# Top-2 gate scaling: groups of 66 and 62 rows per partition in place of 65 and 63

## The chip, the cores and the metric

The kernel runs on one core of one Trainium2 chip. The time is the device time in microseconds (us) of one launch; the figure compared is the median of several runs. Sizes written KB are kibibytes here: a row of `x` is 512 float32 values, or 2 KB, and a row pair of the output is 4 KB.

## The reference

For each of 16 x 1024 tokens there is a row of 512 float32 values and 8 router logits. The two largest softmax probabilities of a token, normalised to sum to one, scale two copies of its row:

```python
probs = np.exp(router_logits - logits_max)
probs = probs / np.sum(probs, axis=-1, keepdims=True)
topk_indices = np.argsort(probs, axis=-1)[..., -k:]
topk_probs = np.take_along_axis(probs, topk_indices, axis=-1)
topk_probs = topk_probs / np.sum(topk_probs, axis=-1, keepdims=True)
x_expanded = x[:, :, np.newaxis, :].repeat(k, axis=2)
return (x_expanded * topk_probs[..., np.newaxis]).astype(np.float32)
```

The smaller of the two weights comes first. With `k = 2` the two weights are the sigmoid of minus and of plus the difference of the two largest logits. 32 MiB of rows come in and 64 MiB go out, so that nearly all of the work is moving data.

## The kernel before

There are 16384 rows, 128 per partition. They are cut into two groups of consecutive rows, `GROUPS = [65, 63]`: in a group of G rows, partition p holds the G consecutive rows from p x G on. A load or store of some rows of a group therefore moves one contiguous run for each of the 128 partitions, and the runs of neighbouring partitions lie G rows apart in memory: 130 KB (G = 65) or 126 KB (G = 63) for loads, twice that, 260 or 252 KB, for stores.

Three buffers lie in the on-chip memory. `xs` has one slot of 2 KB per partition for each row of the larger group. `osp` has `L = 18` slots of 4 KB for row pairs of the output. `WA` holds the weights. A load puts row r of group g into `xs` slot `BASE[g] + r`. A store takes its row pairs either from `osp` or from `xs`: `place` lays the pairs over `xs` slots whose rows have been used, two slots for each pair, so that the multiplication writes partly over its own input.

The list `LOADS` gives the rows of each load, and `STORES` gives for each store its first row, its number of rows, the buffer and the first slot. For each store the main loop issues one VectorE multiplication (line 133), which spreads a row over both weights, and then one store (line 145). Where a store from `osp` slot 0 comes again, its multiplication is cut in two after `FREE[g]` rows: the first part needs only slots that are free early, the second part waits until an earlier store has left the slots behind them.

All loads and all stores but the first go through SyncE's DMA queue (SP), in the order of the program; the first store, of 3 rows, goes through ScalarE's (ACT). SP waits for the multiplication before it issues a store, and for a store to have landed before it issues a load into the same slots. The order on SP is: loads of 2 and 4 rows of group 0, the two loads of logits (lines 125 and 126), the loads of 28 and 31 rows, four stores, the three loads of group 1, four stores. In this document these transfers have names, in the order in which they are issued:

- L1 to L4: the loads of group 0; S0 is the 3-row store on the ACT queue.
- S1 to S4: the stores of group 0 on the SP queue, from rows 3, 18, 34 and 49.
- L5 to L7: the loads of group 1, of 16, 16 and 31 rows. L5 and L6 wait for S2 to have left its `xs` slots, L7 for S4.
- S5 to S8: the stores of group 1, from rows 0, 16, 32 and 47.

The weights come from twelve small VectorE operations on the logits and two ScalarE sigmoids, all in `top2_weights`, which use `osp` as their workspace and are over before the first store.

Of the kernel before, what the change touches and what calls it, by code (L numbers as in the profile page):

```python
# [1 line left out]

# [4 lines left out]

F32 = mybir.dt.float32
ALU = mybir.AluOpType
ACTF = mybir.ActivationFunctionType  # L10
P = 128


def top2_weights(nc, WA, dlt, room, logits, E):

    tt = nc.vector.tensor_tensor
    hi, lo, n = None, None, E  # L20
    while n > 1:
        n //= 2
        if hi is None:
            a, b = logits[:, :, 0:n], logits[:, :, n : 2 * n]
            nhi, nlo = room(n), b
            tt(nhi, a, b, op=ALU.max)  # L26
            tt(nlo, a, b, op=ALU.min)  # L27
        else:
            a, b = hi[:, :, 0:n], hi[:, :, n : 2 * n]
            nhi, nlo, tmp = room(n), room(n), room(n)  # L30
            tt(tmp, lo[:, :, 0:n], lo[:, :, n : 2 * n], op=ALU.max)  # L31
            tt(nlo, a, b, op=ALU.min)  # L32
            tt(nlo, nlo, tmp, op=ALU.max)  # L33
            tt(nhi, a, b, op=ALU.max)  # L34
        hi, lo = nhi, nlo
    tt(dlt, hi[:, :, 0], lo[:, :, 0], op=ALU.subtract)  # L36
    nc.scalar.activation(WA[:, :, 0], dlt, ACTF.Sigmoid, scale=-1.0)  # L37
    nc.scalar.activation(WA[:, :, 1], dlt, ACTF.Sigmoid, scale=1.0)  # L38

GROUPS = [65, 63]

LOADS = [[2, 4, 28, 31], [16, 16, 31]]
BASE = [0, 1]

STORES = [
    [(0, 3, "osp", 0), (3, 15, "osp", 3), (18, 16, "xs", 0), (34, 15, "osp", 0), (49, 16, "xs", 33)],
    [(0, 16, "osp", 2), (16, 16, "xs", 0), (32, 15, "osp", 0), (47, 16, "xs", 32)],
]  # L50

L = 18

FREE = [3, 2]


@with_exitstack
def kernel(
    ctx: ExitStack,
    tc: tile.TileContext,  # L60
    x: bass.AP,
    router_logits: bass.AP,
    k: bass.AP,
    out: bass.AP,
):
    nc = tc.nc
    B, S, D = x.shape
    E = router_logits.shape[-1]
    N = B * S
    assert int(k) == 2 and E == 8 and N == P * sum(GROUPS)  # L70
    M = N // P

    x_v, o_v, rl_v = [], [], []
    t0 = 0
    for n in GROUPS:
        t1 = t0 + P * n
        x_v.append(
            x.rearrange("b s d -> (b s) d")[t0:t1].rearrange("(p m) d -> p m d", p=P)
        )
        o_v.append(  # L80
            out.rearrange("b s k d -> (b s) k d")[t0:t1].rearrange(
                "(p m) k d -> p m k d", p=P
            )
        )
        rl_v.append(
            router_logits.rearrange("b s e -> (b s) e")[t0:t1].rearrange(
                "(p m) e -> p m e", p=P
            )
        )
        t0 = t1  # L90

    wpool = ctx.enter_context(tc.tile_pool(name="wpool", bufs=1))
    xs = wpool.tile([P, max(GROUPS), D], F32)
    osp = wpool.tile([P, L, 2, D], F32)
    WA = wpool.tile([P, M, 2], F32)
    dlt = wpool.tile([P, M], F32)


    flat = osp.rearrange("p l k d -> p (l k d)")
    taken = [0]  # L100

    def room(n):
        o = taken[0]
        taken[0] += M * n
        return flat[:, o : o + M * n].rearrange("p (m n) -> p m n", n=n)

    logits = room(E)

    def place(where, at, n):

        if where == "osp":
            return osp[:, at : at + n]
        return xs[:, at : at + 2 * n, :].rearrange("p (r k) d -> p r k d", k=2)

    m0 = 0
    for g, G in enumerate(GROUPS):
        x0, r = BASE[g], 0
        for n in LOADS[g]:
            tc.keep_in_program_order(
                nc.sync.dma_start(xs[:, x0 + r : x0 + r + n, :], x_v[g][:, r : r + n, :])  # L120
            )
            r += n
            if g == 0 and r == 6:
                n0 = GROUPS[0]
                tc.keep_in_program_order(nc.sync.dma_start(logits[:, :n0], rl_v[0]))  # L125
                tc.keep_in_program_order(nc.sync.dma_start(logits[:, n0:], rl_v[1]))  # L126
                top2_weights(nc, WA, dlt, room, logits, E)
        assert r == G
        for r, n, where, at in STORES[g]:
            og = place(where, at, n)  # L130
            again = where == "osp" and at == 0 and r > 0
            for a, b in [(0, FREE[g]), (FREE[g], n)] if again else [(0, n)]:
                nc.vector.tensor_tensor(  # L133
                    og[:, a:b],
                    xs[:, x0 + r + a : x0 + r + b, :]
                    .unsqueeze(2)
                    .to_broadcast([P, b - a, 2, D]),
                    WA[:, m0 + r + a : m0 + r + b, :]
                    .unsqueeze(3)
                    .to_broadcast([P, b - a, 2, D]),  # L140
                    op=ALU.mult,
                )

            queue = nc.scalar if g == r == 0 else nc.sync
            tc.keep_in_program_order(queue.dma_start(o_v[g][:, r : r + n], og))  # L145
        m0 += G


# [1 line left out]
_INS = ['x', 'router_logits', 'k']  # L150
_OUTS = [((16, 1024, 2, 512), 'float32')]

_NUMBERS = {'k': 2}


# [26 lines left out]
```

## Time and profile before

| what | value |
|---|---|
| median of 3 runs | 240.08 us (239.9 to 240.19) |
| span of the profiled execution, first to last instruction | 238.1 us |
| median less that span | 1.98 us |
| VectorE busy | 141.9 us, 60% of the span |
| bytes read and written | 34.08 MB and 67.11 MB |
| mean over the span | 425 GB/s |

The profile is of one execution, of which it records the span alone; what lies around it is taken as the difference between the median and the span. A line of the profile that names `out_dram<-osp` is a store from `osp`, one that names `xs<-in_x_dram` is a load. "SPq" is the sequencer that issues transfers, and its rows last only as long as the issue. The time from issue to landing holds the time that the transfer stands in the queue behind earlier ones. "DMA share" is the mean busy share of the core's 16 DMA engines; in a short stretch it can go over 1.00, since a packet is counted as a whole.

### The profile page before, as it was taken

The numbers are of one execution on the slowest core, as the hardware profiler recorded it, in microseconds if no ns is written. First come the engines' busy times: TensorE is split into PE (matmuls) and PEld (weight loads), VectorE is DVE, ScalarE is ACT, GpSimd is POOL, SyncE is SP. The second block draws the span as 40 slices with busy tenths as digits, with TensorE's granted clock in tenths as the row PEclk, the third lists the DMA queues.
The fourth block names the chain that finished last, engine by engine and source line by source line (L and its number), as shares of the span: only waits on it lengthen the run. The fifth ranks groups of instructions, "written<-read, shape, count | busy, mean of one in ns | idle before, by whom it ended". The sixth has DMA issues, their size and how long they took to land.

```text
span 238.1 us, 105 instructions
## 1 busy us (share of the span) xinstructions
DVE 141.9 (60%) x22; ACT 1.8 (1%) x3; POOL 0.2 (0%) x4
## 2 busy tenths in 40 slices
DVE  0560499999689999100000799999406999950000
ACT  2000000000000000000000000000000000000000
POOL 0000000000000000000000000000000000000000
DMA  7979998979998999989899999898999989989894
GB/s 249 537 337 526 419 429 376 506 330 495 407 451 363 517 392 434 495 352 528 352 440 440 429 446 491 363 495 374 484 396 418 462 352 506 475 351 517 352 528 176
DMA packets 2593, 101.19 MB, mean 425 GB/s; under 512 B 289, under 2 KB 417, under 8 KB 673
## 3 DMA queue, kind: packets, MB, share of 16 engines
q1 hardware_dynamic: 2448, 99.62, 97.2%
q10 hardware_dynamic: 144, 1.57, 1.5%
q14 instruction: 1, 0.00, 0.0%
HBM read 34.08 MB, written 67.11 MB: 425 GB/s over the span
## 4 chain that ended last, share of the span: by engine, by line
DMA 48%; DVE 40%; SPq 1%; issue 0%; DVEq 0%
DVE osp L133 25%; DMA xs<-in_x_dram 25%; DMA out_dram<-osp 22%; DVE xs L133 14%; SPq L120 0%; SPq L126 0%; SPq L125 0%; SPq L145 0%; DVEq L133 0%
## 5 line engine op out<-in xcount | busy, mean ns | idle before, releaser
L133 DVE TENSOR_TENSOR osp<-xs,WA 128x3072 f32<-128x3072 f32 (+5 forms) x7 | 69.4, 9909 | 61.2 <-DMA xs<-in_x_dram 47.2
L133 DVE TENSOR_TENSOR xs<-xs,WA 128x16384 f32<-128x16384 f32 x4 | 68.9, 17224 | 0.1
L26 DVE TENSOR_TENSOR osp<-osp 128x512 f32<-128x512 f32 x1 | 0.7, 691 | 8.4 <-DMA osp<-in_router_logits_dram 8.4
L37 ACT ACT_TABLE_LOAD x1 | 1.3, 1283 | 0.7 <-PEq L163 0.7
L27 DVE TENSOR_TENSOR osp<-osp 128x512 f32<-128x512 f32 x1 | 0.7, 691 | 0.0
L31 DVE TENSOR_TENSOR osp<-osp 128x256 f32<-128x256 f32 (+1 forms) x2 | 0.7, 350 | 0.0
L32 DVE TENSOR_TENSOR osp<-osp 128x256 f32<-128x256 f32 (+1 forms) x2 | 0.7, 350 | 0.0
L34 DVE TENSOR_TENSOR osp<-osp 128x256 f32<-128x256 f32 (+1 forms) x2 | 0.7, 349 | 0.0
L33 DVE TENSOR_TENSOR osp<-osp 128x256 f32<-128x256 f32 (+1 forms) x2 | 0.7, 348 | 0.0
L37 ACT ACTIVATE WA<-dlt 128x128 f32<-128x128 f32 x1 | 0.3, 314 | 10.3 <-DVE dlt L36 10.3
L36 DVE TENSOR_TENSOR dlt<-osp 128x128 f32<-128x128 f32 x1 | 0.3, 293 | 0.0
L38 ACT ACTIVATE WA<-dlt 128x128 f32<-128x128 f32 x1 | 0.3, 298 | 0.0
L163 POOL MEMSET const-bfloat16-1.0<- 128x1 bf16 x1 | 0.1, 102 | 0.0
L163 POOL MEMSET const-uint8-127<- 128x1 uint8 x1 | 0.1, 101 | 0.0
L163 POOL MEMSET const-float32-0.0<- 128x1 f32 x1 | 0.1, 99 | 0.2 <-issue 0.2
L163 POOL MEMSET const-float32-1.0<- 128x1 f32 x1 | 0.1, 98 | 0.0
## 6 DMA issues: line engine op xcount, KB each, us to landing
out_dram<-osp SPq DMA_DIRECT2D x3, 7680.0 KB, 23.3
xs<-in_x_dram SPq DMA_DIRECT2D x2, 7936.0 KB, 41.3
xs<-in_x_dram SPq DMA_DIRECT2D x2, 4096.0 KB, 40.3
xs<-in_x_dram SPq DMA_DIRECT2D x1, 7168.0 KB, 24.4
out_dram<-osp ACTq DMA_DIRECT2D x1, 1536.0 KB, 26.9
xs<-in_x_dram SPq DMA_DIRECT2D x1, 1024.0 KB, 5.8
xs<-in_x_dram SPq DMA_DIRECT2D x1, 512.0 KB, 3.8
osp<-in_router_logits_dram SPq DMA_DIRECT2D x1, 260.0 KB, 6.0
```

Of the source, the lines that this page charges most:

```text
L26: tt(nhi, a, b, op=ALU.max)
L27: tt(nlo, a, b, op=ALU.min)
L31: tt(tmp, lo[:, :, 0:n], lo[:, :, n : 2 * n], op=ALU.max)
L32: tt(nlo, a, b, op=ALU.min)
L33: tt(nlo, nlo, tmp, op=ALU.max)
L34: tt(nhi, a, b, op=ALU.max)
L36: tt(dlt, hi[:, :, 0], lo[:, :, 0], op=ALU.subtract)
L37: nc.scalar.activation(WA[:, :, 0], dlt, ACTF.Sigmoid, scale=-1.0)
L38: nc.scalar.activation(WA[:, :, 1], dlt, ACTF.Sigmoid, scale=1.0)
L133: nc.vector.tensor_tensor(og[:, a:b], xs[:, x0 + r + a : x0 + r + b, :] .unsqueeze(2) .to_broadcast([P, b - a, 2, D]), WA[:, m0 + r + a : ...
L163: nc = _bacc.Bacc("TRN2", target_bir_lowering=False, num_devices=1)
```

## The change

Only constants at the head of the file change. Group 0 gets 66 rows per partition and group 1 gets 62. L4 loads 32 rows in place of 31 and L7 loads 30 in place of 31. S3 stores 16 rows in place of 15 and S8 stores 15 in place of 16. S4 starts one row later, and lies in `xs` slots 34 to 65 in place of 33 to 64. Group 1 is loaded from `xs` slot 0 on, where it was slot 1. `xs` grows by one slot, 2 KB per partition. The runs of neighbouring partitions now lie 132 and 124 KB apart for loads, 264 and 248 KB for stores. The two loads of logits split at 66 in place of 65. The number and order of instructions and transfers on each engine, and what each waits for, stay as they were; of the multiplications the second part of S3's is one row longer and S8's one row shorter.

```diff
-GROUPS = [65, 63]
+GROUPS = [66, 62]
 
-LOADS = [[2, 4, 28, 31], [16, 16, 31]]
-BASE = [0, 1]
+LOADS = [[2, 4, 28, 32], [16, 16, 30]]
+BASE = [0, 0]
 
 STORES = [
-    [(0, 3, "osp", 0), (3, 15, "osp", 3), (18, 16, "xs", 0), (34, 15, "osp", 0), (49, 16, "xs", 33)],
-    [(0, 16, "osp", 2), (16, 16, "xs", 0), (32, 15, "osp", 0), (47, 16, "xs", 32)],
+    [(0, 3, "osp", 0), (3, 15, "osp", 3), (18, 16, "xs", 0), (34, 16, "osp", 0), (50, 16, "xs", 34)],
+    [(0, 16, "osp", 2), (16, 16, "xs", 0), (32, 15, "osp", 0), (47, 15, "xs", 32)],
 ]
```

## The prediction

> **What bounds the kernel now.** I first read the page's head, then the strip of the DMA engines in 40 slices, the share of each queue, and one long stretch of the table of windows (its last two columns are the DMA share and GB/s).
>
> ```profile
> span 238.1 us, 105 instructions
> DVE 141.9 (60%) x22; ACT 1.8 (1%) x3; POOL 0.2 (0%) x4
> ...
> DMA  7979998979998999989899999898999989989894
> ...
> q1 hardware_dynamic: 2448, 99.62, 97.2%
> q10 hardware_dynamic: 144, 1.57, 1.5%
> ...
> 8.00:232.00 224.00, 141.91 (x22) 0.51 (x2) 0.00 (x0) 1.00 1.00 433
> ```
>
> The reader is to see that the two data queues keep the 16 DMA engines busy for 97.2 + 1.5 = 98.7% of 238.1 us, which is 235.0 us, and that from 8 to 232 us the share is 1.00 at 433 GB/s. VectorE works in 60% of the span. The chain that ended last seems to say something else:
>
> ```profile
> DMA 48%; DVE 40%; SPq 1%; issue 0%; DVEq 0%
> ...
> 194.54 17.22 DVE xs L133
> ```
>
> It gives 40% to VectorE, because it follows one instruction back at a time. Whether those multiplications bind is decided by whether the queue still holds work when each store is issued. For that I put beside the issue times on SP (first column)...
>
> ```profile
> 43.17 0.35 SPq L145 DMA_DIRECT2D out_dram<-osp  x1
> 60.43 0.34 SPq L145 DMA_DIRECT2D out_dram<-xs  x1
> 79.09 0.33 SPq L145 DMA_DIRECT2D out_dram<-osp  x1
> 96.35 0.33 SPq L145 DMA_DIRECT2D out_dram<-xs  x1
> 96.73 26.77 SPq L120 DMA_DIRECT2D xs<-in_x_dram  x3
> 149.96 0.34 SPq L145 DMA_DIRECT2D out_dram<-osp  x1
> 167.22 0.34 SPq L145 DMA_DIRECT2D out_dram<-xs  x1
> 194.53 0.33 SPq L145 DMA_DIRECT2D out_dram<-osp  x1
> 211.79 0.33 SPq L145 DMA_DIRECT2D out_dram<-xs  x1
> ```
>
> ...the time from issue to landing (last column), asked of the view of DMA issues for a short stretch around each issue: S1, S2, S3, S4, L5, L7, S5, S6, S7, S8 from top to bottom.
>
> ```profile
> out_dram<-osp SPq DMA_DIRECT2D x1, 7680.0 KB, 22.9
> out_dram<-xs SPq DMA_DIRECT2D x1, 25.0
> out_dram<-osp SPq DMA_DIRECT2D x1, 7680.0 KB, 24.4
> out_dram<-xs SPq DMA_DIRECT2D x1, 26.8
> xs<-in_x_dram SPq DMA_DIRECT2D x1, 4096.0 KB, 35.9
> xs<-in_x_dram SPq DMA_DIRECT2D x1, 7936.0 KB, 37.9
> out_dram<-osp SPq DMA_DIRECT2D x1, 30.5
> out_dram<-xs SPq DMA_DIRECT2D x1, 32.5
> out_dram<-osp SPq DMA_DIRECT2D x1, 7680.0 KB, 23.3
> out_dram<-xs SPq DMA_DIRECT2D x1, 25.4
> ```
>
> Added up, S1 lands at 66.1, S2 at 85.4, S3 at 103.5, S4 at 123.2, L5 at 132.6, L7 (the last of the three issues that end at 96.73 + 26.77 = 123.5) at about 161.1, S5 at 180.5, S6 at 199.7, S7 at 217.8, S8 at 237.2. I call the time from an issue to the landing of the transfer ahead of it its lead: S2 66.1 - 60.4 = 5.7, S3 85.4 - 79.1 = 6.3, S4 7.1, S5 161.1 - 150.0 = 11.1, S6 13.3, S7 199.7 - 194.5 = 5.2, S8 217.8 - 211.8 = 6.0. How much lead does a gapless queue need? The very first load had nothing ahead of it:
>
> ```profile
> xs<-in_x_dram SPq DMA_DIRECT2D x1, 512.0 KB, 3.8
> ```
>
> 512 KB at 433 GB/s are 1.2 us, so 3.8 - 1.2 = 2.6 us are start and completion. Every lead is twice that or more. The landings confirm it: S1 to S2 is 19.36 us for 16 rows, S7 to S8 again 19.36, S2 to S3 18.06 for 15 rows. So a row pair costs 1.21 us of the queue wherever it stands, and a loaded row half, 0.60. The kernel is bound by bytes, from its first load to its last store.
>
> **The change, part by part.** The sum is made against the span of 238.1 us; the median shown is 1.98 above it.
>
> Bytes: L4 gains a row (+0.60) and L7 loses one (-0.60); S3 gains a row pair (+1.21) and S8 loses one (-1.21). Sum 0.0 us. The number of transfers stays 18, so whatever each costs in itself stays too. The two loads of logits together keep their size, and the first small VectorE operation needs both; I cost this at 0.
>
> What could still cost time is a queue that runs dry, so I follow the new times through. The multiplications, in the table of groups kept apart by shape (mean ns after the count and busy time):
>
> ```profile
> L133 DVE TENSOR_TENSOR xs<-xs,WA 128x16384 f32<-128x16384 f32 x4 | 68.9, 17224 | 0.1
> L133 DVE TENSOR_TENSOR osp<-xs,WA 128x16384 f32<-128x16384 f32 x1 | 17.2, 17226 | 36.4 <-DMA xs<-in_x_dram 36.4
> L133 DVE TENSOR_TENSOR osp<-xs,WA 128x15360 f32<-128x15360 f32 x1 | 16.2, 16158 | 10.8 <-DMA xs<-in_x_dram 10.8
> L133 DVE TENSOR_TENSOR osp<-xs,WA 128x13312 f32<-128x13312 f32 x1 | 14.0, 14026 | 11.1 <-DMA out_dram<-osp 11.1
> L133 DVE TENSOR_TENSOR osp<-xs,WA 128x12288 f32<-128x12288 f32 x1 | 13.0, 12957 | 2.4 <-DMA out_dram<-osp 2.4
> ```
>
> The last two rows differ by one output row: 1.07 us.
>
> - L4 lands 0.6 later. S1 and S2 need rows up to L3 only, so they are issued at 43.2 and 60.4 as before, and land at 66.7 and 86.0; their leads grow by 0.6.
> - S3's second part waits for S1's landing. It starts at 66.7 and takes 14.03 in place of 12.96, so S3 is issued at 80.7, 1.7 later. Its lead is 86.0 - 80.7 = 5.3, down from 6.3. This is the only lead that the change cuts by as much as a microsecond, and S7 shows its like: a 13-row part released by a landing, with a 16-row store ahead, lead 5.2, and S7 still landed 217.83 - 199.72 = 18.11 after S6, without a gap. S3 lands at 86.0 + 19.4 = 105.4.
> - S4's multiplication runs behind S3's on VectorE, to 98.0; lead 7.4. S4 lands at 125.0. L7, behind it on SP, goes out 1.8 later, and L6 ahead of it also runs 1.8 later, so L7's cover is unchanged. L5 and L6 follow S4's issue at once, as before, since S2 has long landed.
> - L5 lands at 134.4. S5 is issued at 151.7; L7, a row shorter, lands at 161.1 + 1.8 - 0.6 = 162.3, lead 10.6. S6 goes out at 169.0, lead 12.7, and S5 lands at 181.7.
> - S7: 181.7 + 14.04 = 195.7, lead 200.9 - 195.7 = 5.2, as before. S8: 15 rows, 195.7 + 16.16 = 211.9, lead 219.0 - 211.9 = 7.1. S8 lands at 219.0 + 18.1 = 237.1 to 237.2, where it lands now.
>
> Everything between L4 and S8 moves back by 0.6 to 1.8 us, and the last transfer, shorter by 1.2, gives it back. The shorter multiplication at the end (-1.07) and the longer one (+1.07) are covered by the queue. If the cover were gone, each would cost or save its microsecond.
>
> One thing has no row of its own: transfers whose runs lie 264 and 248 KB apart (132 and 124 for loads). The nearest rows are the same stores at 260 and 252 KB. The 16-row stores took 19.36 and 19.36; the 15-row ones 18.06 (S3) and 18.11 (S7). Taken at its worst, 0.05 in 18.1 over 235 us of transfers is 0.65 us, of either sign. The issue-to-landing figures are rounded to 0.1, so a difference of two could hide 0.15 in 18.1, which is 1.9 us. I take 0, since the 16-row rows agree to the last digit, and keep -0.65 and +1.9 for the range; a gain of 1.9 is excluded, because the engines already run at 433 GB/s at every pitch that they show. The Trainium skill, "DMA: Bandwidth & Descriptors", section "Where 436 GB/s comes from", puts the ceiling of the 16 ports at 435 GB/s, which the row of 433 bears out.
>
> Sum: 238.1 + 0.0, and 240.08 + 0.0: I forecast 240.1 us, no change that can be measured.
>
> **Rivals.**
>
> *Slower by the pitch.* All pitches become multiples of a power of two twice as large as before, and the stride between partitions could make the engines meet in the same part of memory. It would show in every transfer: the row's 0.05 per 15 rows gives 240.7, the rounding's bound 242.0. It decides from 0.04 us per 15-row store (0.48 us in all). For it: nothing here shows 264 or 248 KB. Against it: no trend from 260 to 252. The same section's page (the Trainium skill, "DMA: Bandwidth & Descriptors", "Latency and other measured facts") reports copies at a pitch of 512 KiB at 207 GB/s against 214 in full, and a pitch padded by 4 KiB at full rate; 264 KB is 8 KB off a power of two, so its loss of 3%, an estimate of 8 us here, is not to be expected, and no run here shows it. Chance 0.21.
>
> *Slower by a dry queue at S3.* Its lead falls to 5.3. From below 2.6 on every microsecond is lost in full; were 5.3 already too little by the 1.0 that it fell, the time would be 241.1. Against it stands S7's gapless 5.2. Chance 0.04.
>
> *Faster at the end.* If S8 began when issued and not when S7 is done, as the chain read by itself suggests, its 15 rows would end 1.2 us sooner: 238.9. Against it: S8 is issued 6.0 us before S7 lands, and all bytes ahead of it must go first. With the pitch's -0.65 (239.4) I give this side 0.09.
>
> **How the numbers follow.** No change has 0.66. 0.2% of 240.08 is 0.48 us, about what a measurement of this kernel can tell. Within it: 0.66; slower 0.21 + 0.04 = 0.25; faster 0.09. The band of no change is 239.6 to 240.6; by itself it holds too little, so the range takes in the pitch's rows: 239.4 to 242.0.
>
> **What would show it.** In the profile after, the stretch from 8 to 232 us should again have a share of 1.00 and 433 GB/s; S3 issued near 80.7, S8 near 211.9 and landing near 237.2; a 16-row store 19.36 after the one ahead, a 15-row store 18.1; the wait of S3's second part ending near 66.7. Longer gaps between all landings would speak for the pitch; one long gap ahead of S3 for the dry queue; S8 landing before 236.5 for the end.

## The result, and the profile after

The changed kernel took 240.66 us (median of 22 runs, 239.94 to 241.87), the kernel before 240.01 us on the same chip (22 runs, 239.72 to 240.79). The ratio is 1.0027, with a 95% interval of 1.0015 to 1.0038: slower by about 0.65 us, a little over the 0.48 us that the prediction had set as the edge of "no change", which the interval (0.36 to 0.91 us) still holds. In two later measurements, beside the experiments below, the ratio was 1.0032 (1.0014 to 1.0050) and 1.0049 (1.0027 to 1.0072).

The page of the changed kernel: span, the strip of the DMA engines, the queues' share.

```profile
span 239.3 us, 105 instructions
DMA  7989999899898989898989999979898989999794
q1 hardware_dynamic: 2448, 99.62, 96.8%
q10 hardware_dynamic: 144, 1.57, 1.5%
```

The span is 1.2 us longer, and yet the big queue did not work longer: 96.8% of 239.3 us is 231.6 us, and it was 97.2% of 238.1 = 231.4 us before. These are sums over 16 engines. So it is not the transfers as a whole that became slower. The issue times of S2, S3, S7 and S8 on SP (first column) and the times from issue to landing (last column, asked around the issues of L1, L3, S2, S3, S7, S8, top to bottom) show where the delay is:

```profile
61.16 0.34 SPq L145 DMA_DIRECT2D out_dram<-xs  x1
81.51 0.33 SPq L145 DMA_DIRECT2D out_dram<-osp  x1
...
196.88 0.33 SPq L145 DMA_DIRECT2D out_dram<-osp  x1
213.08 0.33 SPq L145 DMA_DIRECT2D out_dram<-xs  x1
```

```profile
xs<-in_x_dram SPq DMA_DIRECT2D x1, 512.0 KB, 4.0
xs<-in_x_dram SPq DMA_DIRECT2D x1, 7168.0 KB, 25.1
out_dram<-xs SPq DMA_DIRECT2D x1, 25.6
out_dram<-osp SPq DMA_DIRECT2D x1, 24.6
out_dram<-osp SPq DMA_DIRECT2D x1, 7680.0 KB, 23.4
out_dram<-xs SPq DMA_DIRECT2D x1, 7680.0 KB, 25.3
```

Before, the row of L3 was

```profile
xs<-in_x_dram SPq DMA_DIRECT2D x1, 7168.0 KB, 24.4
```

L1 lands after 4.0 us (3.8 before), L3 after 25.1 (24.4 before), each issued at the same time as before to 0.01 us. So 0.7 us are lost by the end of L3, before any large transfer that the change makes longer or shorter has come up; up to there only the two small loads of logits have other sizes. From there on the stores keep their pace: S2 lands at 86.8 and S3 at 106.1, 19.3 apart for 16 rows; S7 at 220.3 and S8 at 238.4, 18.1 apart for 15 rows. S3 is issued 0.8 later than forecast, S8 1.2 later.

For each transfer the trace holds 16 raises of its semaphore, each behind the last packet of one engine's part, and the landing is the last of the 16. So a transfer lands with the slowest engine. The table of windows shows this for the end: a packet counts where it begins, so the last stretch holds the last packets of late engines alone. Before:

```profile
233.50:234.70 1.20, 0.00 (x0) 0.00 (x0) 0.00 (x0) 1.00 2.02 874
234.70:238.00 3.30, 0.00 (x0) 0.00 (x0) 0.00 (x0) 1.00 0.00 0
```

After:

```profile
233.50:234.70 1.20, 0.00 (x0) 0.00 (x0) 0.00 (x0) 1.00 1.65 717
234.70:238.00 3.30, 0.00 (x0) 0.00 (x0) 0.00 (x0) 1.00 0.09 37
```

Before, every engine had begun its last packet by 234.7 us. After, 37 GB/s over 3.3 us, 120 KB, begin later: two packets of S8, each 60 KB and of one partition. By the 16 raises for S8, fourteen engines were done between 236.8 and 237.2 us, one at 237.5 and the last at 238.3.

### The profile page after: what moved, and what is told of

Read it like the earlier page. It is cut to its first block, busy times and chain, and to the rows that moved or that the text cites. A ratio compares the mean times of both kernels' runs of the same rounds, so it can differ in the third digit from the quotient of the medians.

```text
span 239.3 us, 105 instructions
## 1 busy us (share of the span) xinstructions
DVE 141.9 (59%) x22; ACT 1.8 (1%) x3; POOL 0.2 (0%) x4
## 3 DMA queue, kind: packets, MB, share of 16 engines
q1 hardware_dynamic: 2448, 99.62, 96.8%
q10 hardware_dynamic: 144, 1.57, 1.5%
## 4 chain that ended last, share of the span: by engine, by line
DMA 48%; DVE 40%; SPq 1%; issue 0%; DVEq 0%
DVE osp L133 26%; DMA xs<-in_x_dram 26%; DMA out_dram<-osp 23%; DVE xs L133 14%; SPq L120 0%; SPq L126 0%; SPq L125 0%; SPq L145 0%; DVEq L133 0%
## 5 line engine op out<-in xcount | busy, mean ns | idle before, releaser
L133 DVE TENSOR_TENSOR osp<-xs,WA 128x3072 f32<-128x3072 f32 (+4 forms) x7 | 70.4, 10061 | 62.2 <-DMA xs<-in_x_dram 47.6
L133 DVE TENSOR_TENSOR xs<-xs,WA 128x16384 f32<-128x16384 f32 (+1 forms) x4 | 67.8, 16958 | 0.1
## 6 DMA issues: line engine op xcount, KB each, us to landing
out_dram<-xs SPq DMA_DIRECT2D x1, 7680.0 KB, 25.3
xs<-in_x_dram SPq DMA_DIRECT2D x1, 7168.0 KB, 25.1
```

What stands on the lines that cost most here:

```text
L133: nc.vector.tensor_tensor(og[:, a:b], xs[:, x0 + r + a : x0 + r + b, :] .unsqueeze(2) .to_broadcast([P, b - a, 2, D]), WA[:, m0 + r + a : ...
```

## The experiments

My theory after this result: the distance between the partitions' rows in the *loads* (132 and 124 KB) makes some engine fall behind, and the kernel ends with the slowest. Rivals: the sizes of single transfers, the distance in the stores, or chance on that chip. All ratios are against the kernel before on the same chip, with 95% intervals.

**The change measured again.** No edit.

> The changed kernel itself, beside the others. Every theory: 240.4 to 240.9 us, 0.2 to 0.4% above the kernel before, with a wider spread from run to run. In the trace the work of the DMA queues should again add up as before (97% of the span) while one engine ends about 1 us after the rest.

Measured: 241.22 us (12 runs) against 240.26, ratio 1.0032 (1.0014 to 1.0050). The queue's share was 96.6% of 239.7 = 231.6 us, again the same work in a longer span. The time lay above the 240.9 that was expected, the ratio within its 0.2 to 0.4%. The change is really slower, and chance is out.

**64 and 64 rows.**

```diff
-GROUPS = [65, 63]
+GROUPS = [64, 64]
-LOADS = [[2, 4, 28, 31], [16, 16, 31]]
-BASE = [0, 1]
+LOADS = [[2, 4, 28, 30], [16, 16, 32]]
+BASE = [0, 0]
...
-... (34, 15, "osp", 0), (49, 16, "xs", 33)],
-... (32, 15, "osp", 0), (47, 16, "xs", 32)],
+... (34, 15, "osp", 0), (49, 15, "xs", 34)],
+... (32, 16, "osp", 0), (48, 16, "xs", 32)],
```

> Groups of 64 and 64 rows: partitions 128 KB apart in the loads and 256 KB in the stores, powers of two. If the distance between partitions costs the time (loads or stores), this is worse than 66 and 62: over 240.7 us, and stages of loads or stores below 433 GB/s. If the size of single transfers costs it (a load of 32 rows), about 240.4 to 240.8, since one load of 32 rows is left, in L7. If the change only happened to meet a noisy chip, 240.0.

Measured: 240.74 us, ratio 1.0030 (1.0009 to 1.0052). As slow as 66 and 62, not clearly worse. It is not the same loss, though:

```profile
span 238.9 us, 105 instructions
q1 hardware_dynamic: 2448, 99.62, 97.2%
...
xs<-in_x_dram SPq DMA_DIRECT2D x1, 512.0 KB, 3.7
```

Here the work itself grew, to 97.2% of 238.9 = 232.2 us, by 0.8 us, while L1 landed as early as ever; from 8 to 232 us the engines moved 429 GB/s, where it was 433 before. So these groups cost something too, but elsewhere. Whether that is the power of two in the distance of the loads, of the stores, or the other sizes wasn't taken apart.

**The distance in the loads alone.** Both kernels below take their loads through this helper, with a distance `XP` and a first row `XB` for each group:

```diff
+XP = [66, 62]
+XB = [0, 8384]
...
+    def x_at(g, r, n):
+        a = XB[g] + r
+        return x_rows[a : a + P * XP[g]].rearrange("(p m) d -> p m d", p=P)[:, :n, :]
...
-nc.sync.dma_start(xs[:, x0 + r : x0 + r + n, :], x_v[g][:, r : r + n, :])
+nc.sync.dma_start(xs[:, x0 + r : x0 + r + n, :], x_at(g, r, n))
```

The kernel before with `XP = [66, 62]`:

> The kernel before with its loads alone taking rows 132 and 124 KB apart (so some input rows are other ones, and the output is not the reference's); all transfer sizes and the stores as before. Load distance: 240.6 us, as the change. Transfer sizes or store distance: 240.0 us.

The changed kernel with `XP = [65, 63]` and `XB = [0, 8256]`:

> The changed kernel with its loads alone taking rows 130 and 126 KB apart (the output is not the reference's); all transfer sizes and the stores as changed. Load distance: back to 240.0 us. Transfer sizes or store distance: still 240.6 us.

Measured: the kernel before with the loads' new distance took 240.86 us, ratio 1.0019 (0.9994 to 1.0044; 9 of 12 runs over 240.4, and 14 of 35 of the kernel before beside it). By itself that isn't clear of no change. The changed kernel with the loads' old distance took 239.87 us, ratio 0.9978 (0.9962 to 0.9994), none of 12 runs over 240.4. The second settles it, since its interval lies wholly below that of the change beside it (from 1.0014): with all transfer sizes and the stores' distances of the change, and only the loads as before, nothing is lost. Its end:

```profile
233.50:234.70 1.20, 0.00 (x0) 0.00 (x0) 0.00 (x0) 1.00 1.89 819
234.70:238.00 3.30, 0.00 (x0) 0.00 (x0) 0.00 (x0) 1.00 0.00 0
```

No packet begins after 234.7 us. The stores' 264 and 248 KB and the 64 KB runs of L4 cost nothing that can be measured.

**Other distances, and one group at a time.** The same helper in the changed kernel, with `XP = [67, 61]`:

> The changed kernel with its loads alone taking rows 134 and 122 KB apart (odd numbers of rows, as 130 and 126 were; the output is not the reference's). If it is the power of two in the distance that costs (4 KB in 132 and 124, 2 KB in odd ones): 239.9 us with a narrow spread, as with 130 and 126. If it is how far the distance lies from 130 and 126: 240.6 us or more.

`XP = [66, 63]`:

> The changed kernel with 132 KB in the loads of group 0 and 126 KB in those of group 1 (the output is not the reference's). If the loss arises in both groups, about half of it: 240.2 us, with engines apart by 1 us after L4 but no loss in L7. If only L7 matters: 239.9 us. If only L1 to L4 matter: 240.7 us.

`XP = [65, 62]`:

> The other half: 130 KB in the loads of group 0 and 124 KB in those of group 1 (the output is not the reference's). Loss in both groups: about 240.3 us, from single packets of L7 that take 0.6 to 1 us longer. Only L7: 240.7 us. Only L1 to L4: 239.9 us.

`XP = [68, 60]`:

> Loads 136 and 120 KB apart (multiples of 8 KB; the output is not the reference's). By the power of two: as slow as the change or slower, 240.7 us or more, the next step after 132 and 124. If the even distances next to 64 rows alone are bad: 239.9 us.

| loads, group 0 and 1 | median us | ratio | interval | L1 lands after |
|---|---|---|---|---|
| 134 and 122 KB | 240.08 | 0.9998 | 0.9987 to 1.0010 | 3.6 us |
| 132 and 126 KB | 240.49 | 1.0016 | 0.9989 to 1.0043 | 4.1 us |
| 130 and 124 KB | 239.82 | 0.9989 | 0.9971 to 1.0008 | 3.7 us |
| 136 and 120 KB | 240.50 | 1.0018 | 1.0003 to 1.0032 | 3.7 us |

124 KB in group 1 costs nothing where group 0 is at 130 KB, so the loss needs the loads of group 0. With these alone at 132 KB the runs split: half of the twelve lay between 239.94 and 240.13, half between 240.84 and 242.46. The interval (0.9989 to 1.0043) holds both no loss and the whole loss of the change, so whether 124 KB in group 1 adds to it is not settled here. 134 KB is free, as the odd number of rows was expected to be. 136 KB is a little slower, between the two times that were expected, but with an early L1, so I can't put it down to the same cause, and a rule by powers of two is not what these four show.

**Which loads of group 0.** Two kernels with the loads of the change but for one edit in `x_at` each, the first:

```diff
+        pitch = 65 if g == 0 and r < 6 else XP[g]
-        return x_rows[a : a + P * XP[g]] ...
+        return x_rows[a : a + P * pitch] ...
```

> The changed kernel with L1 and L2 alone (2 and 4 rows) taking rows 130 KB apart, all later loads 132 and 124 KB (the output is not the reference's). If the engines are parted in the first two loads: 239.9 to 240.1 us, L1 landing after 3.8 us as before and not 4.0. If L3 and L4 part them: 240.6 to 241.0 us, as the change.

The second, with `r >= 6` in place of `r < 6`:

> The other half: L1 and L2 132 KB, L3 and L4 130 KB, group 1 124 KB apart (the output is not the reference's). First two loads: 240.6 us, L1 landing after 4.0 us. L3 and L4: 239.9 to 240.1 us.

Beside them, the change itself:

> The changed kernel beside these on the same chip: 240.6 to 241.2 us, as in the two measurements so far.

Measured: with L1 and L2 alone at the old distance 239.96 us, ratio 0.9996 (0.9983 to 1.0010). With L3 and L4 at the old distance and L1 and L2 at 132 KB, 241.16 us, ratio 1.0036 (1.0015 to 1.0057). The change itself 241.58 us, ratio 1.0049 (1.0027 to 1.0072). The last two times lay above what was expected; the order of the three is the one that the first two loads give. So 6 of the 128 rows of a partition, 1.6 MB, decide. The kernel with L1 and L2 at 130 KB, in its page, its issues of S3 and S8 (line 155 of it is line 145 of the kernel before) and the landing of L1:

```profile
span 238.0 us, 105 instructions
q1 hardware_dynamic: 2448, 99.62, 97.2%
```

```profile
80.66 0.33 SPq L155 DMA_DIRECT2D out_dram<-osp  x1
...
211.86 0.33 SPq L155 DMA_DIRECT2D out_dram<-xs  x1
```

```profile
xs<-in_x_dram SPq DMA_DIRECT2D x1, 512.0 KB, 3.7
```

And the change beside it, page, end and L1:

```profile
span 240.2 us, 105 instructions
q1 hardware_dynamic: 2448, 99.62, 96.4%
```

```profile
234.70:238.00 3.30, 0.00 (x0) 0.00 (x0) 0.00 (x0) 1.00 0.13 56
```

```profile
xs<-in_x_dram SPq DMA_DIRECT2D x1, 512.0 KB, 4.0
```

The work is 231.3 and 231.6 us; the spans differ by 2.2 us. In the second, three of S8's packets (56 GB/s x 3.3 us = 180 KB) begin after 234.7. In all six profiles with L1 and L2 at 132 KB and unshifted, L1 landed after 4.0 or 4.1 us; in the seven with another distance, after 3.6 to 3.8. A late L1 doesn't set the size of the loss, though: in the kernel with L1 and L2 at 132 KB and L3 and L4 at 130, the profiled run had L1 after 4.0 and a span of only 238.5 us. It was one of the five of its twelve runs that took 240.0 to 240.3 us.

**Distance or place.** The changed kernel with `XB = [1, 8385]`: every load starts one row further on.

> The changed kernel, every load starting one row (2 KB) further on, the distances 132 and 124 KB kept (the output is not the reference's). If the distance costs the time: 240.6 us or more. If it is where the runs start within 4 KB (all at a multiple of 4 KB with an even distance, half of them with an odd one): another time, up to 239.9 us.

Measured: 240.16 us, ratio 1.0006 (0.9985 to 1.0027), L1 landing after 3.9. The middle lies with the undisturbed kernels, the interval touches that of the change beside it (from 1.0027). It speaks for the place of the runs having a part in it, and doesn't settle it.

## Why the prediction was right or wrong

The range of 239.4 to 242.0 held the time, but the likeliest case, no change within 0.48 us, did not quite come: the loss is about 0.65 us. The case that came is the rival named slower by the pitch, at the time that its first price gave, 240.7; it had a chance of 0.21. It came in another place and another way than that rival said: longer gaps between all landings were to be its sign, and S3 and S8 landed 19.3 and 18.1 us after the stores ahead of them, as forecast. That the price fits is luck: it was a difference of 0.05 us between two stores, spread over all transfers, and the stores turned out to lose nothing.

- *Bytes sum to zero, number of transfers the same.* Right: the queue's work is 231.4 us before and 231.6 after.
- *Leads, and the new times through the kernel.* Right to a tenth, once L1 and L2 are put back: S3 issued at 80.66 (forecast 80.7), S8 at 211.86 (211.9), S8's landing at 211.86 + 25.3 = 237.2 (237.1 to 237.2), span 238.0. The dry queue at S3 did not happen: in the changed kernel itself S3 lands 19.3 us after S2. Nor did an earlier end: S8 landed 18.1 after S7.
- *The pitch costed at 0.* This is the step that failed, and in two ways. It looked at stores, whose rows agreed to the last digit at 260 and 252 KB, and stores are indeed indifferent to 264 and 248; but the same distance halved went into the loads, for which I quoted no pair of rows. And it looked at the pace of whole transfers in the middle of the kernel, where the share was 1.00 before and after. The loss begins in L1 and L2 at the very start, which I had passed over as unchanged because their sizes are, though their addresses moved.
- *A share of 1.00 taken to mean that bytes alone count.* The prediction named the end of the last transfer but priced it as bytes over 433 GB/s. The window from 8 to 232 us did read 1.00 in both kernels (433 and 432 GB/s). That mean hides that the engines need not end together: 0.2 us in the work, 1.2 us in the span.
- *The rule of the Trainium skill* ("DMA: Bandwidth & Descriptors", "Latency and other measured facts") gives rates for pitches from 512 KiB up, and the full rate for a pitch of 4 MiB padded by 4 KiB. I took from it that 8 KB beside a power of two is safe, at a much smaller pitch, of which it says nothing. For the stores at 264 KB, of which I said it, that held. For the loads the runs don't bear it out: with L1 and L2 at 132 KB, which is 4 KB off 128, the kernel was slow, at 130 and 134 KB it was not, and at 128 KB itself L1 landed early (3.7 us).

The landings say that the loss is made in two parts, one by the end of L3 and one about L7: S1's landing, forecast at 66.7, released S3's second part at 67.46; S5's, forecast at 181.7, released S7's at 182.83. These two rows of the changed kernel's timeline carry that:

```profile
67.46 14.03 DVE L133 TENSOR_TENSOR osp<-xs,WA 128x13312 f32<-128x13312 f32 x1 [3.05 <-DMA out_dram<-osp]
182.83 14.03 DVE L133 TENSOR_TENSOR osp<-xs,WA 128x13312 f32<-128x13312 f32 x1 [10.99 <-DMA out_dram<-osp]
```

How a late L1 (0.2 us) becomes 0.7 and then 1.2 us can be followed in the 16 semaphore raises of each transfer. From the first to the last of them it is, in us:

| transfer | before | the change | the change, L1 and L2 at 130 KB |
|---|---|---|---|
| L1 | 0.56 | 0.84 | 0.44 |
| L3 | 0.62 | 1.44 | 0.38 |
| S3 | 0.39 | 0.98 | 0.39 |
| L6 | 0.46 | 0.96 | 0.46 |
| L7 | 0.46 | 1.44 | 0.43 |
| S8 | 0.50 | 1.57 | 0.42 |

The engines that were parted in L1 are parted further in L3, come a little closer again by the first stores, and are parted once more in L7; the stores pass on what they get. At the same 132 and 124 KB, but with the engines together after L1 (last column), L3 and L7 add nothing. Nor is it the 124 KB: with group 0 at 132 KB and L7 at 126 KB the spread went from 0.94 after L6 to 1.37 after L7. These are single profiles, and L3 parted the engines in one quick kernel too: with all loads at 130 and 126 KB from 0.54 to 0.94, which was down to 0.43 after L4. In L7 it is in the main one packet, the last of the engine that was already the last. A stretch of 0.2 us at 307 GB/s holds one packet of 60 KB, and its share times 16 engines times 0.2 us is the time that this packet took. The rows are L7's last packet to begin in the changed kernel, in its third measurement, and with L1 and L2 at 130 KB:

```profile
160.10:160.30 0.20, 0.20 (x1) 0.00 (x0) 0.00 (x0) 1.00 0.90 307
...
160.40:160.60 0.20, 0.20 (x1) 0.00 (x0) 0.00 (x0) 1.00 1.11 307
...
159.40:159.60 0.20, 0.20 (x1) 0.00 (x0) 0.00 (x0) 1.00 0.76 307
```

That is 2.9, 3.6 and 2.4 us, where the middle one of all packets of this size took 2.27. In all three profiles of the change the engine of this packet, followed from packet to packet, is the one that ends the kernel. In the first it ran to 163.1 us, when the other engines had been done with L7 for 0.5 us or more and went on to S5. That a late engine loses more because it still loads while the others store fits this, but is argued, not tried. What parts the engines further in L3 stays open.

## What to carry to other kernels

In this kernel the DMA engines were busy all the time, and the end was set by the slowest of them. In one like it, compare the queue's work (share times span) with the span, and look at which packets begin last, before calling a kernel bound by bytes alone. A change of tiling moves the addresses of every transfer, also of those whose size it leaves alone; price the first, small loads by themselves. To tell sizes from addresses, let one kernel keep the sizes and take other addresses.

## What the runs showed that I had not expected

Two loads of 2 and 4 rows, 1.6 MB of 101, moved the whole time by 0.3 to 0.5%, and nothing later made up for it: the spread between the engines was 0.98 us at S3 and 1.57 at S8. S8's 128 packets lie in the trace in 16 rows of eight that follow each other without a gap, so an engine that comes late to a store has as much to do as the others, and ends late. The time of the changed kernel also varies more: 239.88 to 243.07 us in 11 runs of it, 239.78 to 240.32 in 12 runs of the same sizes with loads at 130 and 126 KB. The kernel before also varies more than the latter: 239.82 to 242.12 us in the 35 runs beside it. Why 132 KB and not 128, 130, 134 or 136 delays L1 stays open. The kernel with the changed sizes and loads at 130 and 126 KB was faster than the one before (0.9978), but it reads other rows than the task asks for, and no run here has that gain with the right rows.
